# A decoder layer on one core: attention's key copied out of its accumulators by ScalarE, scaled and rotated in SBUF behind the inverse's first update

## The chip, the cores and the metric

The kernel runs on one core of one Trainium2 chip. The metric is the time of one execution on the device in microseconds (us), the median of several runs. Beside the timed runs there is one profiled execution, whose trace gives the start and length of each instruction on each engine: PE (TensorE, matmuls; PEld is its weight load), DVE (VectorE), ACT (ScalarE), POOL (GpSimd) and SP (SyncE, which here issues DMAs). PE writes its results into accumulators in PSUM, eight banks of 128 partitions by 512 float32; DVE and ACT read them there.

## What is computed

One layer of a hybrid decoder on a sequence of 256 tokens of width 1024, in float32. An RWKV-7 branch and a softmax attention branch take the same normalised input and are merged by gates; a gated MLP follows.

```python
h = rms_norm(x, norm1_g)
proj = h @ w_in                                  # one combined projection
y_a = rwkv7_time_mix(token_shift(proj[:RWKV_IN]), ...)
q, k, v = heads of proj[RWKV_IN:RWKV_IN + 3 * 512]     # 8 heads of 64
q = partial_rope(rms_norm(q, q_norm_g), positions)     # rotates 16 of 64 columns
k = partial_rope(rms_norm(k, k_norm_g), positions)
y_b = causal_attention(q, k, v)
x = x + (sigmoid(gate_a) * (y_a @ w_branch_a) + sigmoid(gate_b) * (y_b @ w_branch_b)) @ w_out
x = x + conv_ffn(rms_norm(x, norm2_g), ...)
```

In the RWKV branch a state of 64 by 64 per head is updated for each token by a decay and a rank-one correction. The change touches only the key `k` of the attention, between its projection and its use; what is computed stays the same.

## The kernel before

**Weights.** Every weight tile of 128 by 1024 passes through three steps: SP loads it into `raw` (4 buffers), ACT rounds it into `whi` (L262, a CAST, 4 buffers), DVE takes the rest `wlo` = `raw` - `whi` (L272, 3 buffers). PE multiplies the two halves apart (L300, L302 and L305, or L321, L322 and L325) to keep float32 accuracy. These steps stand in the queues of ACT and DVE between all other work.

**Two threads.** The middle of the kernel is written as generators that a small planner at L1200 interleaves by costs and delays: `bulk` issues the projections, gates and branch products, `chain` the RWKV branch, and `att` the attention (from the moment its inputs are issued). Within an engine instructions run in the order in which they stand in its queue; code inside `tc.high_priority()` is moved ahead of code that isn't, and `tc.issue_after(i)` keeps an instruction behind another in the order.

**The inverse.** The RWKV recurrence is taken in chunks of 64 tokens, for each of which a triangular 64 by 64 matrix is inverted (16 pairs of head and chunk per half of the partitions). The inverses of its 16 by 16 blocks are made on DVE and spread by DMAs into `X0` and, transposed, `X`. Then PE doubles the block size twice. First `pp` = G times X0 (L844), copied to `P` by ACT and DVE (L850, L851); `px` = X times P (L858), added into `X0` on DVE with four instructions (L864): this is the inverse's first update. Then `pxt` (L872), in two halves, gives the same for `X`, which ACT copies (L880); `pp` (L886), `pxt` (L897) make the second doubling. Between these pieces the planner puts gate tiles (L300 to L305) and the attention's transposes (`pqk`, L1052), one piece of work each.

**The key.** `attention_input(i)` projects query (i = 0), value (2) and key (1) into two accumulators of 128 tokens by 512 each. For the key the first comes from the tag `acc` and the second from the tag `ch` (3 buffers), from which `px`, `pxt` and `pp` take theirs too. `finish_qk(p, i, t)` is then called for both halves t of the tokens: ACT squares the accumulator into `s2` (L1016), DVE sums per head into `r2` (L1019), and, for the key, DVE and POOL make the inverse root (L1021, L1022); DVE multiplies the accumulator by it into `qkv` (L1026) and rotates 16 columns by six small instructions (two `ro` at L1035, L1037 and L1038 among them). The accumulator is free when L1026 has read it. `attention()` turns query and key with `pqk` on PE, four transposes at a time, twice for the query and then twice for the key, each time copied out by ACT (L1053).

Of the kernel before, what the change touches and what calls it, by code (L numbers as in the profile page):

```python
# [13 lines left out]
OP = mybir.AluOpType  # L14
# [22 lines left out]
def body(tc, x, positions, norm1_g, w_in, rwkv_mu, w_decay_up, decay_bias, w_aaa_up,  # L37
# [3 lines left out]
    act, dve, pool, pe = nc.scalar, nc.vector, nc.gpsimd, nc.tensor  # L41
    ctx = ExitStack()
    with ctx:
# [12 lines left out]
        def b4(name, shape=(128, 4, 256), dt=F32):  # L56
            return sb.tile(list(shape), dt, name=name, tag="b4", bufs=NB4)
# [53 lines left out]
        rowf = cst.tile([128, 1], F32, name="rowf")  # L111
# [450 lines left out]
        def chain():  # L562
# [45 lines left out]
            p = chp("pss")  # L608
# [15 lines left out]
            for ct in range(4):  # L624
                dve.scalar_tensor_tensor(kk[:, ct], zk[:, ct], col(KK_ + ct), pr[ct],
                                         op0=OP.mult, op1=OP.mult)
# [205 lines left out]
            def quad(side, h):  # L832
                return slice(64 * side + 32 * h, 64 * side + 32 * h + 32)
# [26 lines left out]
            for a in range(2):  # L860
                for q in range(2):
                    v = X0[quad(1 - q, 0), 8 * a:8 * a + 8, 0:16]
                    with tc.high_priority():
                        dve.scalar_tensor_tensor(v, px[a][quad(1 - q, 0)], rowf[quad(1 - q, 0)], v,  # L864
                                                 op0=OP.mult, op1=OP.add)
            yield 0.6, 2.5
            pt = chp("pxt")[:, 0:256].rearrange("p (u n) -> p u n", n=16)
            for h in range(2):
# [136 lines left out]
        qkv = {}  # L1005
        ybs = []
        inv_last = []

        def finish_qk(p, i, t):

            d = qkv[i][:, t]
            if i == 2:
                act.copy(d.rearrange("p h n -> p (h n)"), p)
                return
            s2 = b2("s2", [128, 512])
            act.activation(s2, p, AF.Square)  # L1016
            r2 = sb.tile([128, 8], F32, name="r2", tag="r2", bufs=2)
            with tc.high_priority():
                dve.tensor_reduce(r2, s2.rearrange("p (h n) -> p h n", h=8), axis=AX.X, op=OP.add)  # L1019
                if i:  # L1020
                    dve.tensor_scalar(r2, r2, 1.0 / N, NORM_EPS, op0=OP.mult, op1=OP.add)  # L1021
                    pool.tensor_tensor(r2, r2, eps1[:, 1:2].to_broadcast([128, 8]), op=OP.pow)  # L1022
                else:
                    act.activation(r2, r2, AF.Sqrt, scale=1.0 / N, bias=eps1[:, 0:1])
                    dve.reciprocal(r2, r2)
                dve.tensor_tensor(d, p.rearrange("p (h n) -> p h n", h=8),  # L1026
                                  r2[:, :, None].to_broadcast([128, 8, 64]), op=OP.mult)
            ro = sb.tile([128, 2, 2, 8, HALF], F32, name="ro", tag="ro", bufs=2)
            en = dve
            y = [d[:, :, 0:HALF], d[:, :, HALF:ROT]]  # L1030
            with ExitStack() as st:
                if inv_last:
                    st.enter_context(tc.issue_after(inv_last[-1]))
                for f in range(2):
                    en.tensor_tensor(ro[:, f], y[f][:, None].to_broadcast([128, 2, 8, HALF]),  # L1035
                                     rot[:, i, t, f][:, :, None, :].to_broadcast([128, 2, 8, HALF]), op=OP.mult)
                en.tensor_tensor(y[0], ro[:, 0, 0], ro[:, 1, 0], op=OP.subtract)  # L1037
                en.tensor_tensor(y[1], ro[:, 1, 1], ro[:, 0, 1], op=OP.add)  # L1038
# [4 lines left out]
        def attention():  # L1043
            qkT = []
            for i in range(2):
                dT = b4(f"qkT{i}")
                for j in range(2):
                    p = atp("pqk").rearrange("p (a t c) -> p a t c", a=2, t=2)
                    for a in range(2):
                        for t in range(2):  # L1050
                            ct = 2 * j + a
                            pe.transpose(p[:, a, t], flat3(qkv[i][:, t])[:, ct * 128:ct * 128 + 128], ident)  # L1052
                    act.activation(dT[:, 2 * j:2 * j + 2].rearrange("p a c -> p (a c)"),  # L1053
                                   p.rearrange("p a t c -> p (a t c)"), AF.Copy, scale=gcol[:, i:i + 1])
                    yield 0.4, 1.0
                    while not joined[0] and "chain" not in done:
                        yield 0, 0.1
                qkT.append(dT)
            qT, kT = qkT


            sc0 = by("sc", (128, 8, 128))
            sc1 = cst.tile([128, 2112], F32, name="sc1", tag="KB")[:, 0:2048].rearrange("p (h k) -> p h k", k=256)
            parts = ((0, 0, 8, sc0), (1, 0, 4, sc1[:, 0:4]), (1, 1, 4, sc1[:, 4:8]))

            def scores(t, j, nh, sc):
                nk = 128 * (t + 1)
                ts = slice(t * 128, t * 128 + 128)
                pq = [atp("ps").rearrange("p (h k) -> p h k", k=nk) for q in range(2)]
                for i in range(nh // 2):  # L1070

                    for q, hs in PAR:
                        pe.matmul(pq[q][:, i], qT[hs, 2 * j + i, ts], kT[hs, 2 * j + i, 0:nk],
                                  start=True, stop=True)
                for q in range(2):
                    dve.tensor_tensor(sc[:, q:nh:2, nk - 128:nk], pq[q][:, :, nk - 128:nk],
                                      cmask[:, None, :].to_broadcast([128, nh // 2, 128]), op=OP.add)
                    if t:
                        act.copy(sc[:, q:nh:2, 0:128], pq[q][:, :, 0:128])

            def softmax(t, j, nh, sc):
                nk = 128 * (t + 1)
                mx = sb.tile([128, nh], F32, name="mx", tag="mx", bufs=2)
                dve.tensor_reduce(mx, sc, axis=AX.X, op=OP.max)
                dve.tensor_scalar(mx, mx, -0.125, None, op0=OP.mult)
                sm = sb.tile([128, nh], F32, name="sm", tag="sm", bufs=2)
                for h in range(nh):
                    act.activation(sc[:, h], sc[:, h], AF.Exp, scale=0.125, bias=mx[:, h:h + 1],
                                   accum_out=sm[:, h:h + 1])
                dve.reciprocal(sm, sm)  # L1090
                dve.tensor_tensor(sc, sc, sm[:, :, None].to_broadcast([128, nh, nk]), op=OP.mult)

            def turned_w(t, j, nh, sc):

                pTs = []
                for g in range(2):
                    pp = atp("ppt")
                    pT = b2("pT", [128, 512])
                    for i in range(4):
                        h, b = g * nh // 2 + i // (t + 1), i % (t + 1)  # L1100
                        pe.transpose(pp[:, i * 128:i * 128 + 128], sc[:, h, b * 128:b * 128 + 128], ident)
                    act.copy(pT, pp)
                    pTs.append(pT)
                return pTs

            def weighted(t, pTs):

                po = atp("po").rearrange("p (i c) -> p i c", i=4)
                for ct in range(4):
                    for b in range(t + 1):  # L1110
                        for q, hs in PAR:
                            n = (2 * ct + q) * (t + 1) + b
                            pe.matmul(po[hs, ct], qkv[2][:, b, 2 * ct + q],
                                      pTs[n // 4][:, n % 4 * 128:n % 4 * 128 + 128],
                                      start=ct + b == 0, stop=ct == 3 and b == t, skip_group_check=True)
                hv = ybh[:, :, t * 128:t * 128 + 128]
                act.copy(hv, po)
                dve.tensor_tensor(ybl[:, :, t * 128:t * 128 + 128], po, hv.bitcast(F32), op=OP.subtract)


            for i, part in enumerate(parts):
                scores(*part)
                yield 0.9, 2.5
                softmax(*part)
                while i < 2 and not joined[0] and "chain" not in done:
                    yield 0, 0.1
            yield 0, 4.0
            ybh = by("ybh", dt=F32R)
            ybl = by("ybl", dt=F32R)
            p0 = turned_w(*parts[0])  # L1130
            yield 0.9, 2.5
            weighted(0, p0)
            pa = turned_w(*parts[1])
            yield 1.8, 3.0
            pb = turned_w(*parts[2])
            yield 0.9, 2.5
            weighted(1, pa + pb)
            yield 1.9, 2.5
            ybs.extend((ybh, ybl))
# [254 lines left out]
```

## Time and profile before

| what | value |
|---|---|
| timed runs, median | 409.33 us (409.2 to 409.97, 3 runs) |
| the profiled execution | 410.96 us |
| its span, from first to last instruction | 409.0 us |
| granted TensorE clock, mean over the span | 0.996 of full speed |
| weight CASTs on ACT (L262) | 122 of 1052 ns, 127.8 us |
| weight rests on DVE (L272) | 122 of 1228 ns, 149.4 us |

The span lies 1.96 us below the profiled execution's own time; that rest is ahead of the first and behind the last instruction. A row of a timeline has the start and the length in us, the engine, the line, the operation, its output and inputs, the shape and a count; brackets hold the idle time of the engine just before it and what ended that. In a view of waits the columns are the total in us, how many times, and the longest. The chain of waits is followed back from the last instruction, at each step to what released it. A row of windows has a stretch of the span, its length, the busy time of engines with a count of instructions, the granted clock of TensorE as a share of full speed, the busy share of the DMA engines and GB/s. A row of one line's instructions has the least, the middle and the greatest duration in ns. Buffer numbers are left out of names, so `X` stands for both `X0` and `X`, and `r` and `s` for `r2` and `s2`.

### The profile page before, as it was taken

Reading aid. Unit: us, or ns where it says so; the run is one execution under the profiler, and the core shown is the slowest. Engines: PE = TensorE matmul, PEld = TensorE weight load, DVE = VectorE, ACT = ScalarE, POOL = GpSimd, SP = SyncE. Lnnn points to the kernel's source line nnn. Section 1 sums busy time; section 2 is a strip of 40 time slices with the busy share of each in tenths; the row PEclk is TensorE's granted clock in tenths of the full one; section 3 lists DMA queues with packets and bytes.
Section 4 is the critical chain, followed back from the end, with each engine's and each line's share of the span. In section 5 each row is a group of like instructions: output and inputs, shape, how many; then the busy total and the mean of one; then the engine's idle time right before and its main releaser. Section 6 shows DMA issues by size and latency. Waiting matters only on the chain.

```text
span 409.0 us, 8287 instructions
## 1 busy us (share of the span) xinstructions
PE 401.1 (98%) x3282; PEld 349.6 (85%) x3282; DVE 316.9 (77%) x537; ACT 232.8 (57%) x391; POOL 44.4 (11%) x72
## 2 busy tenths in 40 slices
PE   7999999999989999999999999999999999999996
PEld 3899899887889898999988888888888888888885
DVE  3878999769464798677965898968769678697794
ACT  6999666365436776543554864635545555464450
POOL 8810610213220010000000000000000000000000
PEclk9999999999989999999999999999999999999999
DMA  8973557645825333636665547566655666656612
GB/s 244 325 233 103 169 147 204 163 124 141 223 57 158 101 104 106 206 113 200 192 200 172 159 156 216 190 205 174 222 178 167 209 191 199 195 173 204 198 57 104
DMA packets 60193, 70.35 MB, mean 172 GB/s; under 512 B 7608, under 2 KB 50506, under 8 KB 60154
## 3 DMA queue, kind: packets, MB, share of 16 engines
q1 hardware_dynamic: 59222, 69.40, 57.0%
q0 software_dynamic: 880, 0.41, 0.6%
q8 instruction: 26, 0.43, 0.4%
q14 instruction: 13, 0.11, 0.1%
q10 hardware_dynamic: 52, 0.01, 0.0%
HBM read 68.37 MB, written 1.44 MB: 171 GB/s over the span
## 4 chain that ended last, share of the span: by engine, by line
PE 82%; DVE 6%; DMA 5%; issue 2%; ACT 2%; POOL 1%; SPq 1%; DVEq 0%; ACTq 0%; POOLq 0%
PE acc L1275 20%; PE acc L1280 10%; PE acc L300 7%; PE acc L305 6%; PE acc L302 6%; PE f L1297 4%; PE f L1299 4%; PE f L1295 4%; PE acc L321 3%; PE acc L325 3%; PE acc L322 3%; PE idle L465 1%; DMA raw<-in_w_in_dram 1%; DMA x<-in_x_dram 1%; DMA Tb<-d 1%
## 5 line engine op out<-in xcount | busy, mean ns | idle before, releaser
L262 ACT CAST whi<-raw 128x1024 fp32r<-128x1024 f32 x122 | 127.8, 1052 | 116.5 <-PE acc L1275 40.3
L272 DVE TENSOR_TENSOR wlo<-raw,whi 128x1024 fp32r<-128x1024 f32 x122 | 149.4, 1228 | 40.6 <-PE acc L1280 14.1
L1275 PE MATMUL acc<-hx,whi 128*128 128x512 f32 x352 | 89.5, 395 | 0.0
L1275 PEld LDWEIGHTS acc<-hx,whi 128*128 128x128 f32 x352 | 63.4, 188 | 12.4
L300 PE MATMUL acc<-hx,whi 128*128 128x256 f32 x224 | 57.9, 292 | 0.0
L302 PE MATMUL acc<-hx,whi 128*128 128x256 f32 x224 | 55.4, 282 | 0.0
L1280 PEld LDWEIGHTS acc<-hx,wlo 128*128 128x128 f32 x352 | 46.8, 188 | 4.0
L1280 PE MATMUL acc<-hx,wlo 128*128 128x256 f32 x352 | 47.3, 277 | 0.0
L300 PEld LDWEIGHTS acc<-hx,whi 128*128 128x128 f32 x224 | 43.0, 192 | 2.5 <-issue 1.4
L302 PEld LDWEIGHTS acc<-hx,whi 128*128 128x128 f32 x224 | 42.9, 192 | 0.1
L305 PE MATMUL acc<-hx,wlo 128*128 128x256 f32 x224 | 35.4, 281 | 0.0
L1297 PE MATMUL f<-whi,hb 128*128 128x512 f32 x80 | 31.2, 390 | 0.0
L1299 PE MATMUL f<-wlo,hb 128*128 128x512 f32 x80 | 31.2, 390 | 0.0
L1295 PE MATMUL f<-whi,hb 128*128 128x512 f32 x80 | 31.2, 389 | 0.0
L305 PEld LDWEIGHTS acc<-hx,wlo 128*128 128x128 f32 x224 | 30.4, 191 | 0.0
L1285 DVE TENSOR_REDUCE an<-acc 128x256 f32<-128x512 f32 x22 | 14.2, 686 | 9.4 <-PE acc L1280 9.3
L321 PE MATMUL acc<-whi,hx 128*128 128x512 f32 x48 | 19.5, 406 | 0.0
L322 PE MATMUL acc<-whi,hx 128*128 128x512 f32 x48 | 18.8, 392 | 0.0
L1299 PEld LDWEIGHTS f<-wlo,hb 128*128 128x128 f32 x80 | 15.0, 188 | 3.1
L1297 PEld LDWEIGHTS f<-whi,hb 128*128 128x128 f32 x80 | 15.0, 188 | 2.8
L1295 PEld LDWEIGHTS f<-whi,hb 128*128 128x128 f32 x80 | 15.0, 188 | 2.8
L325 PE MATMUL acc<-wlo,hx 128*128 128x512 f32 x48 | 14.9, 392 | 0.0
(326 smaller groups left out, 621.9 us busy)
## 6 DMA issues: line engine op xcount, KB each, us to landing
raw<-in_w_ffn_up_dram SPq DMA_DIRECT2D x44, 512.0 KB, 4.3
raw<-in_w_in_dram SPq DMA_DIRECT2D x41, 512.0 KB, 4.2
raw<-in_w_ffn_down_dram SPq DMA_DIRECT2D x22, 512.0 KB, 3.4
raw<-in_w_out_dram SPq DMA_DIRECT2D x8, 512.0 KB, 4.5
x<-in_x_dram SPq DMA_DIRECT2D x8, 256.0 KB, 3.9
raw<-in_w_branch_b_dram SPq DMA_DIRECT2D x4, 512.0 KB, 4.2
raw<-in_w_branch_a_dram SPq DMA_DIRECT2D x4, 512.0 KB, 3.5
out_dram<-o SPq DMA_DIRECT2D x3, 256.0 KB
```

What stands on the lines that cost most here:

```text
L262: act.copy(hi[:, :k * c], raw[:, :k * c])
L272: eng.tensor_tensor(lo[:, :n], raw[:, :n], hi[:, :n].bitcast(F32), op=OP.subtract)
L300: pe.matmul(om, wh[:, k, ms], xh[:, k0 + k], start=k0 + k + m == 0, stop=False, skip_group_check=True)
L302: pe.matmul(om, wh[:, k, ms], xl[:, k0 + k], start=False, stop=False, skip_group_check=True)
L305: pe.matmul(om, wl[:, k, ms], xh[:, k0 + k], start=False, stop=k0 + k == nk - 1 and m == n - 1, skip_group_check=True)
L321: pe.matmul(ps_[t], xh[:, K, ts], wh[:, k], start=K == 0, stop=False)
L322: pe.matmul(ps_[t], xl[:, K, ts], wh[:, k], start=False, stop=False)
L1275: pe.matmul(ps_[m], wh[:, k, m * 128:m * 128 + 128], hx[:, k0 + k].rearrange("p a s -> p (a s)"), start=k0 + k == 0, stop=False, skip_grou ...
L1280: pe.matmul(ps_[m][:, 0:S], wl[:, k, m * 128:m * 128 + 128], hh[:, k0 + k], start=False, stop=k0 + k == 7, skip_group_check=True)
L1295: pe.matmul(fin[f], hb[:, 0, i, ts], wh[:, 0, cs], start=st, stop=False, skip_group_check=f == 3)
L1297: pe.matmul(fin[f], hb[:, 1, i, ts], wh[:, 0, cs], start=False, stop=False, skip_group_check=f == 3)
L1299: pe.matmul(fin[f], hb[:, 0, i, ts], wl[:, 0, cs], start=False, stop=False, skip_group_check=f == 3)
```

## The change

For the key, ACT copies each accumulator as it is into `qkv`, right behind the square. The multiply by the inverse root and the rotation are put off: a list `later` keeps them, and `key_scaled()` issues them from `qkv` in SBUF, in place, behind the last of the four instructions of the inverse's first update (or ahead of the key's first turn in `attention()`, if the chain has not come there). The rotation becomes a function of its own; for the query it now stands inside the block with high priority.

```diff
-                        dve.scalar_tensor_tensor(v, px[a][quad(1 - q, 0)], rowf[quad(1 - q, 0)], v,
-                                                 op0=OP.mult, op1=OP.add)
+                        x0_last.append(dve.scalar_tensor_tensor(v, px[a][quad(1 - q, 0)], rowf[quad(1 - q, 0)], v,
+                                                                op0=OP.mult, op1=OP.add).ins)
+            key_scaled()
...
+        later, x0_last = [], []
...
-                dve.tensor_tensor(d, p.rearrange("p (h n) -> p h n", h=8),
-                                  r2[:, :, None].to_broadcast([128, 8, 64]), op=OP.mult)
+                if i:
+                    act.copy(d.rearrange("p h n -> p (h n)"), p)
+                else:
+                    dve.tensor_tensor(d, p.rearrange("p (h n) -> p h n", h=8),
+                                      r2[:, :, None].to_broadcast([128, 8, 64]), op=OP.mult)
+                    rotate(i, t)
+            if i:
+                later.append((t, r2))
+
+        def key_scaled():
+            for t, r2 in later:
+                with tc.issue_after(x0_last[-1]):
+                    dve.tensor_tensor(qkv[1][:, t], qkv[1][:, t], r2[:, :, None].to_broadcast([128, 8, 64]),
+                                      op=OP.mult)
+                rotate(1, t)
+            later.clear()
+
+        def rotate(i, t):
+            d = qkv[i][:, t]
...
             for i in range(2):
+                if i:
+                    key_scaled()
                 dT = b4(f"qkT{i}")
```

On PE nothing moves. What changes there is what the first half of `pxt` waits for, behind the gate tile that uses the accumulator `acc`. Before:

```order
L305 MATMUL acc<-hx,wlo 128x256 x4
L872 MATMUL pxt<-X,P 16x16 [waits DVE_49,Activation_49]
L872 MATMUL pxt<-X,P 16x16 x31
L1052 MATMUL pqk<-ident,qkv 128x128 x4
L300 MATMUL acc<-hx,whi 128x256
```

Now (the lines of the changed kernel lie 1 to 21 further down):

```order
L305 MATMUL acc<-hx,wlo 128x256 x4
L873 MATMUL pxt<-X,P 16x16 [waits Activation_49]
L873 MATMUL pxt<-X,P 16x16 x31
L1073 MATMUL pqk<-ident,qkv 128x128 x4
L300 MATMUL acc<-hx,whi 128x256
```

The wait for DVE, whose last multiply read the accumulator, is gone; the wait for ACT stays and is now for the second copy.

On ACT, behind the copy of `P`, the two squares `s` of the key stood together; `r` and `s` carry their numbers here, one for each half of the tokens. Before:

```order
L850 COPY P<-pp 128x128 [waits PE_49]
L1016 ACTIVATE s_1476<-acc 128x512
L1016 ACTIVATE s_1488<-acc 128x512
L262 CAST whi<-raw 128x1024 [waits DMAHW3_49,DVE_49,PE_49]
L1053 ACTIVATE qkT_1572<-pqk,gcol 128x512 [waits DMASW0_49,DMASW1_49,PE_49,Pool_49]
```

Now:

```order
L850 COPY P<-pp 128x128 [waits PE_49]
L1018 ACTIVATE s_1476<-acc 128x512
L1029 COPY qkv<-acc 128x512
L1018 ACTIVATE s_1483<-acc 128x512
L1029 COPY qkv<-acc 128x512
L262 CAST whi<-raw 128x1024 [waits DMAHW3_49,DVE_49,PE_49]
L1074 ACTIVATE qkT_1574<-pqk,gcol 128x512 [waits DMASW0_49,DMASW1_49,PE_49,Pool_49]
```

Two copies have come in, ahead of the weight CAST and the first turned query.

On DVE, from the inverse root's first scaling to the key's last rotation; `X_1127` is `X0`. Before:

```order
L1021 TENSOR_SCALAR r_1490<-r_1490 128x8 [waits DVE_49]
L1026 TENSOR_TENSOR qkv<-acc,r_1478 128x512 [waits Pool_49]
L1026 TENSOR_TENSOR qkv<-acc,r_1490 128x512 [waits Pool_49]
L1035 TENSOR_TENSOR ro<-qkv,rot 128x128 [waits DVE_49]
L1035 TENSOR_TENSOR ro<-qkv,rot 128x128
L864 SCALAR_TENSOR_TENSOR X_1127<-px,rowf,X_1127 32x8x16 [waits DMASW3_49,PE_49]
...
L1035 TENSOR_TENSOR ro<-qkv,rot 128x128 x2
L272 TENSOR_TENSOR wlo<-raw,whi 128x1024 [waits DMAHW2_49]
L1037 TENSOR_TENSOR qkv<-ro 128x8x8 [waits DVE_49]
L1038 TENSOR_TENSOR qkv<-ro 128x8x8
L272 TENSOR_TENSOR wlo<-raw,whi 128x1024 [waits DMAHW3_49,PE_49,Activation_49]
```

Now:

```order
L1023 TENSOR_SCALAR r_1485<-r_1485 128x8 [waits DVE_49]
L272 TENSOR_TENSOR wlo<-raw,whi 128x1024 [waits DMAHW2_49,PE_49]
L864 SCALAR_TENSOR_TENSOR X_1127<-px,rowf,X_1127 32x8x16 [waits DMASW3_49,PE_49,Pool_49]
...
L1040 TENSOR_TENSOR qkv<-qkv,r_1478 128x512 [waits Pool_49]
L1040 TENSOR_TENSOR qkv<-qkv,r_1485 128x512 [waits Activation_49,Pool_49]
L1054 TENSOR_TENSOR ro<-qkv,rot 128x128 [waits DVE_49]
...
L1054 TENSOR_TENSOR ro<-qkv,rot 128x128
L272 TENSOR_TENSOR wlo<-raw,whi 128x1024 [waits DMAHW3_49,PE_49,Activation_49]
L1056 TENSOR_TENSOR qkv<-ro 128x8x8 [waits DVE_49]
L1057 TENSOR_TENSOR qkv<-ro 128x8x8
```

A weight rest and the four updates of `X0` have moved ahead of the two multiplies, and a second weight rest stands ahead of the last two instructions of the rotation. The update's wait for POOL, new in its row, is for the early clearing of `X0`. At the query, the six instructions of the second half's rotation stand ahead of a shift of `zv` that two of them stood behind.

## The prediction

> **What bounds the kernel now.** I read the page first, then PE's waits, the chain of waits, and the timelines of PE, DVE and ACT around the one place that stands out.
>
> ```profile
> PE 401.1 (98%) x3282; PEld 349.6 (85%) x3282; DVE 316.9 (77%) x537; ACT 232.8 (57%) x391; POOL 44.4 (11%) x72
> PEclk9999999999989999999999999999999999999999
> ```
>
> PE is busy for 98% of the span and its clock drops in one slice only, the twelfth (112.5 to 122.7 us). So time can be won only where PE stands still or runs slowly. The view of PE's own waits, by total us, times and the longest, has three rows and no more:
>
> ```profile
> PE xt L426 <- DVE xn L419: 1.6, 2, 0.8
> PE pxt L872 <- DVE qkv L1026: 1.5, 1, 1.5
> PE idle L387 <- DVE eps L382: 1.5, 1, 1.5
> ```
>
> The first and third lie in the first 9 us. The second is the only named wait after the start: the first matmul of `pxt` (L872) waits for the multiply L1026 that scales the attention key out of its accumulator, since `pxt` takes over that accumulator's bank. The chain of waits shows how the multiply comes to be late:
>
> ```profile
> 108.64 1.05 ACT whi L262
> 109.69 0.16 ACT P L850
> 109.85 0.51 ACT s L1016
> 110.38 1.28 DVE r L1019 x2
> 111.83 3.30 POOL r L1022 x2
> 115.15 0.70 DVE qkv L1026
> ```
>
> Square on ACT, two sums on DVE, two powers in a row on POOL (3.30 us), then the second multiply, which ends at 115.85. PE had come to `pxt` at 114.50:
>
> ```profile
> 115.99 0.97 PE L872 MATMUL pxt<-X,P 32*16 32x16 f32 x64 [1.49 <-DVE qkv L1026]
> 116.89 0.98 PE L1052 MATMUL pqk<-ident,qkv 128*128 128x128 f32 x4
> 117.52 0.56 PE L300 MATMUL acc<-hx,whi 128*128 128x256 f32 x1
> ...
> 121.86 0.97 PE L872 MATMUL pxt<-X,P 32*16 32x16 f32 x64
> 122.75 0.66 PE L1052 MATMUL pqk<-ident,qkv 128*128 128x128 f32 x4
> 123.17 0.36 PE L300 MATMUL acc<-hx,whi 128*128 128x256 f32 x1
> ...
> 126.09 0.75 PE L886 MATMUL pp<-X,G 32*32 32x32 f32 x64
> ```
>
> The same three pieces (one half of `pxt`, four turns `pqk`, one gate weight tile) stand there twice. The first set takes 121.86 - 115.99 = 5.87 us, the second 126.09 - 121.86 = 4.23. The windows say why:
>
> ```profile
> 116.00:117.00 1.00, 1.00 (x65) 1.00 0.00 0
> 117.00:118.00 1.00, 1.00 (x6) 0.54 0.06 16
> 118.00:119.00 1.00, 1.00 (x7) 0.50 0.00 0
> 119.00:120.00 1.00, 1.00 (x6) 0.50 0.00 0
> 120.00:121.00 1.00, 1.00 (x8) 0.75 0.63 52
> ```
>
> The columns are stretch, length, PE busy, granted clock, DMA share and GB/s. The clock is halved from 117.0 to about 120.5; its loss is 0.46 + 0.50 + 0.50 + 0.25 = 1.71 us, close to 5.87 - 4.23 = **1.64**, which I use. So this wait costs **1.49 us idle and, in this execution, 1.64 us of clock behind it**.
>
> **The change, part by part.** *The wait goes.* The accumulators are now read by four ACT instructions in a row, square, copy, square, copy, and `pxt` waits for ACT alone. The copy of this shape from an accumulator exists already for the value, and the squares start 0.49 us apart:
>
> ```profile
> L1013 ACT COPY qkv<-acc x2: 580/583/586, 83.1 to 85.0; 128x512 f32<-128x512 f32 x2
> 109.75 1.09 ACT L1016 ACTIVATE s<-acc 128x512 f32<-128x512 f32 x2
> ```
>
> Four steps of 0.49 from 109.75 and a last tail end the second copy near 111.8. PE wants the bank at 114.50: 2.7 us to spare. Minus 1.49 us. No table load is added between square and copy.
>
> *The clock dip goes with it.* From 114.5 PE then has a half of `pxt`, four turns and dense tiles without a gap, as at 121.86 to 126.09, where no slot of the clock row shows a loss. Minus 1.64.
>
> *ACT, two copies more.* They delay what is queued behind them, two weight CASTs with a turned query between:
>
> ```profile
> 110.71 1.06 ACT L262 CAST whi<-raw 128x1024 fp32r<-128x1024 f32 x1
> 114.08 1.04 ACT L262 CAST whi<-raw 128x1024 fp32r<-128x1024 f32 x1 [1.55 <-PE acc L302]
> ```
>
> The delay is 2 x 0.49 = 1 us, and it ends at the second CAST, ahead of which ACT sat idle 1.55 us for PE. The first CAST feeds a weight tile that PE reaches two tiles after `pxt`. So it costs nothing; without that cover it would cost the 1 us.
>
> *DVE, new order.* What decides is when the key is scaled and rotated, since PE turns it (third `pqk`, at 122.75 now). The rows:
>
> ```profile
> 110.38 1.28 DVE L1019 TENSOR_REDUCE r<-s 128x8 f32<-128x512 f32 x2 [2.03 <-ACT s L1016]
> 115.76 0.48 DVE L1035 TENSOR_TENSOR ro<-qkv,rot 128x128 f32<-128x128 f32 x2
> 116.28 1.23 DVE L864 SCALAR_TENSOR_TENSOR X<-px,rowf,X 32x128 f32<-32x128 f32 x4
> 117.43 0.20 DVE L1037 TENSOR_TENSOR qkv<-ro 128x64 f32<-128x64 f32 x1
> 118.10 1.21 DVE L272 TENSOR_TENSOR wlo<-raw,whi 128x1024 fp32r<-128x1024 f32 x1
> L1022 POOL TENSOR_TENSOR r<-r,eps x2: 1633/1652/1672, 111.8 to 113.5; 128x8 f32<-128x8 f32 x2
> L1026 DVE TENSOR_TENSOR qkv<-acc,r x4: 627/680/691, 61.4 to 115.2; 128x512 f32<-128x512 f32 x4
> L1091 DVE TENSOR_TENSOR sc<-sc,sm x3: 1216/1226/1228, 139.9 to 153.4; 128x1024 f32<-128x1024 f32 x3
> ```
>
> The second sum now waits for a square that starts 0.49 later, so both sums and their scalings end near 112.2. A weight split `wlo` (1.21) comes next, whose operands are there, to 113.3; then the four updates of the inverse (1.23), to 114.5. The powers follow their own sums: 111.2 + 1.65 = 112.9 and + 1.65 = 114.5, so neither multiply waits for POOL by more than a moment. A multiply of this shape from SBUF is not in the trace: 0.69 is the same multiply from the accumulator (L1026), 0.61 is half of the softmax's in-place multiply of twice the width (L1091). I take 0.69, the row of the same length; two of them run to about 115.8. Then come three of the four rotations `ro` (0.26 each: two from 115.76 to the update at 116.28), two combinations, the fourth `ro`, a second `wlo` and the last two combinations: 115.8 + 0.8 + 0.3 + 0.3 + 1.1 + 0.3 = **118.6**, or 118.4 at the low price of the multiplies. PE arrives at the third `pqk` at 114.5 + 5.1, namely its half of `pxt`, turns, tile (4.23) and second half (0.89): 114.50 + 4.23 + 0.89 = **119.6**. The key is ready 1.0 to 1.2 us early. Cost nothing; if that margin is gone, each us late costs one us.
>
> *The updates of the inverse* start at 113.3 in place of 116.28; their reader (L886 at 126.09) did not wait, so nothing is won. The weight split moved ahead of them frees a weight buffer 5 us sooner; PE waits for no load there, so nothing either. POOL and SP keep their order. *The query's rotation*, at 62 to 65 us, moves two small combinations ahead of a `zv` shift, about 0.3 us by their spacing above; PE has no wait in that stretch: nothing.
>
> *Does the gain reach the end?*
>
> ```profile
> 121.00:225.00 104.00, 103.86 (x1169) 94.33 (x1169) 76.31 (x132) 60.04 (x125) 4.93 (x4) 1.00 0.52 157
> 225.00:400.00 175.00, 175.00 (x939) 150.04 (x938) 142.64 (x213) 95.18 (x138) 0.70 (x1) 1.00 0.59 181
> ACT whi L262 <- PE acc L1275: 40.3, 28, 1.8
> ```
>
> After 121 us PE is idle for 0.14 us up to 400, DMA is half used, and the weight CASTs wait for PE, not the other way round. A PE that runs 3 us earlier pulls all of it along.
>
> Sum: 1.49 + 1.64 = 3.13 us, on the profiled execution 410.96 (span 409.0 and 1.96 around it): 407.8. That execution lies 1.63 us above the median of the timed runs, 409.33. On the median the sum gives **406.2**. But 1.63 is also just the size of the clock term, and that leaves a doubt: the profiled execution may have had a dip that the timed ones do not have.
>
> **The rivals.** *Only the wait goes.* The dip begins a full microsecond after PE has resumed, so it is granted by some count over a stretch whose phase I do not see; the idle 1.49 us and tiny matmuls fell together in 113.6 to 117.0 here. If the timed runs have no dip, or it also comes without the wait, the gain is 1.49: **407.8**. For it: the 1.63 us between profile and median. Against it: three timed runs within 0.8 us, and no dip behind the later `pxt` and turns.
>
> By the Trainium skill, page "TensorE: Matmul & The Clock Gate", Part 1 on the clock gate, the clock halves after an idle window of about 3.4 us, in a window that runs free of the kernel. The length of the dip, 117.0 to 120.5, agrees with such a window; its cause does not, since 1.49 us idle came before it. By that rule the wait had not been long enough, and the sum would be 1.49 alone, as in this rival.
>
> *A new wait takes the place of the old one, and the kernel is slower.* The place is the third `pqk`: between the key's two rotations DVE now has a weight split that waits for its load and its CAST, and behind it the last rotation. Were that held for W us beyond PE's arrival at 119.6, PE would pay W, and from about 1.5 us on the clock dip of 1.64 again. It passes the old time when W + 1.64 is over 3.13, so from W = 1.5: the key ready at 121.1, 2.5 us later than worked out. At W = 2.5 the time is 406.2 + 2.5 + 1.64 = **410.3**. Against it: that CAST ran at 110.71 already, so its load had landed, and POOL is done by 114.5.
>
> *The change does not do what it says*: `pxt` stands at the same place because of something else that becomes ready near 116, or the gain is taken back before 225 us. Then **409.3**. Against it: the copies are done 2.7 us ahead, and the view of PE's waits has nothing later.
>
> **How the numbers follow.** Both terms go: 0.53, at 406.2 (its own range 405.5 to 407.0). Only the wait: 0.29, at 407.8. No effect: 0.11, at 409.3. Slower: 0.07, at 410.3. The range 405.5 to 408.3 takes in the first two cases and leaves out 0.18; the low end allows 0.7 for the multiplies' price and the spread of runs. A difference of 0.2%, 0.8 us, is about what a measurement can tell: faster than 408.5 has 0.83, between that and 410.1 0.11, slower 0.06.
>
> **What would show it.** Right: PE has no wait at `pxt` and the clock row shows no slot below 9; the first `pxt` starts within 0.1 of the end of the tile ahead of it; the second copy on ACT ends near 112; the last key combination on DVE ends near 118.6, PE's third `pqk` starts near 119.6; the span is about 405.9. Wrong: a wait of PE on the key's combination at the third `pqk`; a dip of the clock that stays although the wait is gone (the second term falls); or a later idle time of PE of about the size won.

## The result and the profile after

The changed kernel takes **407.67 us** (median of 22 runs, 406.48 to 408.66). The kernel before, run beside it 22 times, takes 409.76 (407.39 to 412.80). The ratio is **0.9946, with a 95% interval of 0.9930 to 0.9963**: faster by 0.54%, or 2.1 us between the medians. The profiled execution took 407.20 us, with a span of 405.1 and a mean granted clock of 1.000; before it was 410.96, 409.0 and 0.996.

The page of the changed kernel, its engines and its row of the granted clock:

```profile
PE 399.6 (99%) x3282; PEld 347.9 (86%) x3282; DVE 316.9 (78%) x537; ACT 233.8 (58%) x393; POOL 44.6 (11%) x72
...
PEclk9999999999999999999999999999999999999999
...
PE 98%; DMA 1%; DVE 0%; issue 0%; ACT 0%; SPq 0%
```

No slot of the clock is below 9 now, and the third line, the chain of work by engine, is 98% PE. The whole view of PE's waits (total us, times, longest):

```profile
PE idle L387 <- DVE eps L382: 1.5, 1, 1.5
PE xt L426 <- DVE xn L419: 0.7, 1, 0.7
```

Both lie in the start-up. The wait at `pxt` is gone, and nothing has taken its place. The timeline of PE from the inverse's first update to the second doubling:

```profile
109.80 0.73 PE L858 MATMUL px<-P,X 32*32 32x16 f32 x64
...
113.78 0.97 PE L873 MATMUL pxt<-X,P 32*16 32x16 f32 x64
114.68 0.66 PE L1073 MATMUL pqk<-ident,qkv 128*128 128x128 f32 x4
...
118.00 0.97 PE L873 MATMUL pxt<-X,P 32*16 32x16 f32 x64
118.90 0.66 PE L1073 MATMUL pqk<-ident,qkv 128*128 128x128 f32 x4
...
122.22 0.75 PE L887 MATMUL pp<-X,G 32*32 32x32 f32 x64
```

From the first `pxt` to the second PE now takes 4.22 us, as from the second to `pp`; before, the first of these stretches took 5.87. From `px` to `pp` it takes 12.42 us. Before it took 15.65, from `px` at 110.44 to `pp` at 126.09, so 3.23 us are gone here. The other 0.64 us of the 3.9 by which the span is shorter lie ahead of `px` (110.44 against 109.80). Of these, 0.37 come from the start-up (its first gate tile, L300, starts at 17.76 before and at 17.39 now; the waits of `xt` there were 1.6 us and are 0.7), the rest in small parts between 102 and 110 us, all of it ahead of the key's first copy (109.95).

ACT and DVE in the same place:

```profile
108.35 1.05 ACT L262 CAST whi<-raw 128x1024 fp32r<-128x1024 f32 x1 [5.02 <-DMA raw<-in_w_in_dram]
109.31 0.26 ACT L850 COPY P<-pp 128x128 f32<-128x128 f32 x1
109.46 0.60 ACT L1018 ACTIVATE s<-acc 128x512 f32<-128x512 f32 x1
109.95 0.59 ACT L1029 COPY qkv<-acc 128x512 f32<-128x512 f32 x1
110.42 0.62 ACT L1018 ACTIVATE s<-acc 128x512 f32<-128x512 f32 x1
110.91 0.61 ACT L1029 COPY qkv<-acc 128x512 f32<-128x512 f32 x1
```

```profile
111.87 1.22 DVE L272 TENSOR_TENSOR wlo<-raw,whi 128x1024 fp32r<-128x1024 f32 x1
113.13 1.22 DVE L864 SCALAR_TENSOR_TENSOR X<-px,rowf,X 32x128 f32<-32x128 f32 x4
114.28 1.27 DVE L1040 TENSOR_TENSOR qkv<-qkv,r 128x512 f32<-128x512 f32 x2
...
117.83 0.20 DVE L1057 TENSOR_TENSOR qkv<-ro 128x64 f32<-128x64 f32 x1
```

The second copy ends at 111.52, 2.26 us ahead of `pxt`. The two multiplies from SBUF take 1.27 us together, 0.64 each, between the two bounds of 0.61 and 0.69. The key is ready at 118.03, and PE turns it at 118.90: 0.87 us to spare.

So in the two profiled executions the place itself went as worked out, 3.23 us for 3.13. In the timed runs the gain is 2.1. The first row of ACT above points to the reason, and the kernel before has the same row, of which the prediction did not follow the wait. Here it is, with the piece of the chain of waits that stands ahead of the pieces shown there:

```profile
103.09 5.44 DMA raw<-in_w_in_dram
```

```profile
108.64 1.05 ACT L262 CAST whi<-raw 128x1024 fp32r<-128x1024 f32 x1 [4.94 <-DMA raw<-in_w_in_dram]
```

ACT stood idle for 4.94 us on the load of a weight tile. The copy of `P` and the key's squares, whose inputs were there, stood behind that CAST in ACT's queue. The chain that ended in the wait at `pxt` began with a load.

### The profile page after: what moved, and what is told of

The parts are those of the page before. It is cut to its first block, busy times and chain, and to the rows that moved or that the text cites. A ratio compares the mean times of both kernels' runs of the same rounds, so it can differ in the third digit from the quotient of the medians.

```text
span 405.1 us, 8289 instructions
## 1 busy us (share of the span) xinstructions
PE 399.6 (99%) x3282; PEld 347.9 (86%) x3282; DVE 316.9 (78%) x537; ACT 233.8 (58%) x393; POOL 44.6 (11%) x72
## 4 chain that ended last, share of the span: by engine, by line
PE 98%; DMA 1%; DVE 0%; issue 0%; ACT 0%; SPq 0%
PE acc L1296 20%; PE acc L1301 10%; PE acc L300 9%; PE acc L302 8%; PE acc L305 8%; PE acc L321 5%; PE acc L325 5%; PE acc L322 5%; PE f L1318 5%; PE f L1316 4%; PE f L1320 4%; PE idle L465 1%; PE pgr L681 1%; DMA x<-in_x_dram 1%; PE ppt L1122 1%; PE ps L1094 1%
## 5 line engine op out<-in xcount | busy, mean ns | idle before, releaser
L262 ACT CAST whi<-raw 128x1024 fp32r<-128x1024 f32 x122 | 127.8, 1051 | 114.4 <-PE acc L1296 39.5
L1296 PEld LDWEIGHTS acc<-hx,whi 128*128 128x128 f32 x352 | 63.4, 188 | 12.4
L300 PE MATMUL acc<-hx,whi 128*128 128x256 f32 x224 | 56.9, 289 | 0.0
L302 PE MATMUL acc<-hx,whi 128*128 128x256 f32 x224 | 54.6, 279 | 0.0
L300 PEld LDWEIGHTS acc<-hx,whi 128*128 128x128 f32 x224 | 42.2, 188 | 2.5 <-issue 1.4
L302 PEld LDWEIGHTS acc<-hx,whi 128*128 128x128 f32 x224 | 42.2, 189 | 0.1
```

The lines of the kernel that those rows point to most:

```text
L262: act.copy(hi[:, :k * c], raw[:, :k * c])
L300: pe.matmul(om, wh[:, k, ms], xh[:, k0 + k], start=k0 + k + m == 0, stop=False, skip_group_check=True)
L302: pe.matmul(om, wh[:, k, ms], xl[:, k0 + k], start=False, stop=False, skip_group_check=True)
L1296: pe.matmul(ps_[m], wh[:, k, m * 128:m * 128 + 128], hx[:, k0 + k].rearrange("p a s -> p (a s)"), start=k0 + k == 0, stop=False, skip_grou ...
```

## The experiments

Three sets of runs. The first and the third ran on one chip, the second on another; on which chip the comparison above ran is not known. In the expectations A is the prediction's account: the wait of 1.49 us is always there, and the clock falls because of it. E, formed after the first set, is the late load. The other accounts are told where they are named.

### First set: which part of the change does it, and what does a wait cost

**Copies without the deferral.** The accumulators are copied as in the changed kernel, but multiply and rotation stay where they were, reading SBUF.

```diff
-                dve.tensor_tensor(d, p.rearrange("p (h n) -> p h n", h=8),
-                                  r2[:, :, None].to_broadcast([128, 8, 64]), op=OP.mult)
+                if i:
+                    act.copy(d.rearrange("p h n -> p (h n)"), p)
+                    src = d
+                else:
+                    src = p.rearrange("p (h n) -> p h n", h=8)
+                dve.tensor_tensor(d, src, r2[:, :, None].to_broadcast([128, 8, 64]), op=OP.mult)
```

> The two copies alone: the accumulator is freed by ScalarE, the key is scaled in SBUF as soon as its power is there, and nothing is put off by hand. Theory A (the wait costs 1.49 us in every execution, the halved clock 1.64 us more only in some executions): no wait at the first pxt, clock 1.00 in all runs, the same time as the changed kernel, about 2.1 us below the kernel before. Theory B (both terms are lost in every execution, and 1 us is given back by putting the multiply off): 3.1 us below. Theory C (the deferral itself made the gain): no gain.

**The second half first, no copies.** The key's halves are finished in the other order, so that the accumulator which `pxt` takes over is read first.

```diff
-                for t in range(2):
+                for t in (1, 0) if i == 1 else (0, 1):
```

> No copies at all. The two halves of the key are finished in the other order, so that the half whose bank pxt takes gets its power and its multiply first, 1.65 us sooner. Theory A: the multiply ends near 114.2 on the scale of the profile of before, PE comes at 114.5 and does not wait; clock 1.00 in all runs; about 2.1 us below the kernel before, the same as the changed kernel. Theory B with the give-back in ScalarE's two copies: 3.1 us below. Theory C (the copies and the new order matter, not the wait): no gain.

**One more power.** The kernel before, with an unused power on POOL ahead of the second half's own: the wait is to grow by its 1.65 us.

```diff
+                    if t:
+                        r3 = sb.tile([128, 8], F32, name="r3")
+                        pool.tensor_tensor(r3, r2, eps1[:, 1:2].to_broadcast([128, 8]), op=OP.pow)
```

> The kernel before with one more power on GpSimd (1.65 us, its result unused) ahead of the second half's power: PE's wait at pxt grows from 1.49 to about 3.14 us. Theory A: the clock is halved in nearly every run (mean clock 0.996 or less in most), and the time grows by 1.65 us and by the share of the 1.64 us that the kernel before did not pay, together about 2.6 us above the kernel before. Theory B (the clock is always halved already): 1.65 us above. Theory D (the timed runs see no halved clock): 1.65 us above with a clock of 1.00.

**A short wait.** Halves in the other order and an unused power of half the width in front.

```diff
-                    pool.tensor_tensor(r2, r2, eps1[:, 1:2].to_broadcast([128, 8]), op=OP.pow)
+                    with ExitStack() as st:
+                        if t:
+                            r3 = sb.tile([128, 4], F32, name="r3")
+                            pool.tensor_tensor(r3, r2[:, 0:4], eps1[:, 1:2].to_broadcast([128, 4]), op=OP.pow)
+                        else:
+                            st.enter_context(tc.issue_after(pow_last[-1]))
+                        pow_last.append(pool.tensor_tensor(r2, r2, eps1[:, 1:2].to_broadcast([128, 8]), op=OP.pow).ins)
...
-                for t in range(2):
+                for t in (1, 0) if i == 1 else (0, 1):
```

> As the run with the second half first, with a power of half the width (1.0 us by its row, its result unused) ahead of that half's power: PE's wait at pxt is about 0.75 us. Theory A: the clock is halved in fewer runs than in the kernel before, or in none; 0.75 us plus at most a small share of 1.64 above the run with no wait, so about 1.2 us below the kernel before. Theory B (any wait here halves the clock): 0.75 + 1.64 above the run with no wait, 0.7 us below the kernel before or no gain.

Measured, beside a kernel before that took **407.51** here (33 runs), not 409.76:

| kernel | median us | against before, 95% | PE's wait at `pxt` in its profile |
|---|---|---|---|
| copies, no deferral | 407.72 | 0.9999 (0.9990 to 1.0008) | none |
| second half first | 407.45 | 0.9992 (0.9975 to 1.0010) | none |
| one more power | 409.13 | 1.0038 (1.0021 to 1.0056) | 1.31 |
| a short wait | 407.56 | 1.0002 (0.9991 to 1.0013) | 1.20 |

On this chip the kernel before was as fast as the changed one had been, and the copies alone, or the other order of the halves, won nothing. That is the number of C, and A and B both missed; but C's reason does not follow, since the whole change wins nothing here either (the second and third set show it). The extra power shows why. In its profile, PE's wait at `pxt` is

```profile
PE pxt L872 <- DVE qkv L1029: 1.3, 1, 1.3
```

1.31 us, where an addition of 1.65 to 1.49 had been expected to give 3.14. By that estimate PE would not have waited here without the power, by 1.65 - 1.31 = 0.34 us. **A's fixed wait fell at this run.** (The time lies 409.13 - 407.51 = 1.62 us above the kernel before, where B and D had said 1.65. That agreement is luck: both had started from a wait of 1.49 in every run.) The CAST ahead of the squares, in the timeline of the same kernel, says what was different:

```profile
106.13 1.05 ACT L262 CAST whi<-raw 128x1024 fp32r<-128x1024 f32 x1 [2.76 <-DMA raw<-in_w_in_dram]
```

It starts at 106.13, where before's profile has 108.64. The short wait gives the other case. Its profiled execution took 410.57 us, and all its 12 other runs took 406.86 to 408.61. In that one execution:

```profile
108.93 1.05 ACT L262 CAST whi<-raw 128x1024 fp32r<-128x1024 f32 x1 [5.37 <-DMA raw<-in_w_in_dram]
```

The same load, late again, and a wait with it. (The view of waits names a gate of ACT there, but the multiply of the second half ends at 115.60, 0.15 us ahead of `pxt` at 115.75, the same step as from 115.84 to 115.99 in before's profile. 0.75 us had been expected, for an early load.) The time from the load's issue on SP to the CAST is 5.55 us in the profile of before, 5.66 in that of the changed kernel and 6.16 here. In the other three of this set it is 4.10, 4.07 and 4.06. That is theory E: **the kernel before waits at `pxt` in executions in which this one load lands late, and in no others.** So far it rests on these profiles, one of each kernel.

### Second set: the load made late on purpose

Four spare scatters of 16 KB, of data that nothing uses, are put in SP's queue right ahead of the load, in the kernel before and in the changed one:

```diff
+            spare = sb.tile([128, 16, 16], F32, name="spare")
+            for b in range(4):
+                nc.sync.dma_start(spare[16 * b:16 * b + 16], d3[2 * b].rearrange("q u (i n) -> i (q u) n", i=16))
```

> The kernel before with four more scatters of 16 KB, into a spare tile, in SyncE's queue ahead of that weight load (their data are not used): the load is issued about 1.9 us later, so its CAST on ScalarE starts near 108.3 where it would start near 106.2. Theory E: PE's wait at pxt appears in most runs, 1.2 to 2 us, with the halved clock in some; median 1.5 to 3 us above a kernel before whose load is early. Theory A: the load is not what the wait hangs on; no change beyond 0.3 us.

> The changed kernel with the same four scatters ahead of the weight load. Theory E: the copies end 2.7 us ahead of PE, so a load that is 2 us late is still hidden; no wait at pxt, at most a few tenths at px, whose operand is copied behind the same CAST; 1.5 to 3 us below the kernel before with the late load, within 0.5 us of the changed kernel without it. Theory A: the same as the changed kernel.

The third kernel is before with the same scatters and no copies. The weight CASTs that stood ahead of the copy of `P` and of the squares are put behind them in ACT's queue:

```diff
-        def split_hi():
+        def split_hi(after=None):
...
+                with ExitStack() as st:
+                    if after:
+                        st.enter_context(tc.issue_after(after[-1]))
...
-            act.activation(s2, p, AF.Square)
+            sq_last.append(act.activation(s2, p, AF.Square).ins)
...
-                yield from xst(ps_, hh, hl)
+                yield from xst(ps_, hh, hl, hold=i == 1)
...
+                if i == 1:
+                    split_hi(sq_last)
```

(`hold` keeps back the last tile's CAST until the squares are issued.)

> The kernel before with the late load, and no copies: instead ScalarE's CAST of that weight tile and the one ahead of it stand behind the copy of P and the key's two squares. Theory E: the key's chain no longer waits for the load; squares near 107 us on PE's scale, no wait at pxt though the load is as late as in the other two runs; the time of the changed kernel. If the wait is still there, something other than the load's place in ScalarE's queue holds the squares.

And the changed kernel once more as it is:

> The changed kernel once more, beside the kernel before on the chip of this call. Theory E (new: the wait of 1.49 us is there only when one weight tile lands late, near 108.4 us of the span, and gone when it lands near 106.2): the gain depends on how often the load is late here; 2.1 us as in the first comparison where most executions of the kernel before span over 407 us, and nothing where they span 405 to 406. Theory A (the wait is always there): 1.5 us at least, on any chip.

The kernel before took 407.65 us on this chip (29 runs, 406.28 to 410.59).

| kernel | median us (range) | against before, 95% |
|---|---|---|
| before, late load | 411.93 (410.69 to 412.53) | 1.0110 (1.0089 to 1.0131) |
| changed, late load | 408.43 (406.80 to 409.19) | 1.0025 (1.0008 to 1.0043) |
| before, late load, CASTs behind | 408.13 (407.17 to 408.53) | 1.0013 (1.0002 to 1.0025) |
| changed, as it is | 407.60 (407.07 to 408.05) | 1.0000 (0.9983 to 1.0016) |

The kernel before with its load made late has the wait again, now in its profile and, by time and clock, in all six runs. The profile, first PE's wait, then PE's row, then the windows behind it (PE busy, granted clock, DMA share and GB/s):

```profile
PE pxt L874 <- DVE qkv L1028: 2.0, 1, 2.0
```

```profile
115.45 0.97 PE L874 MATMUL pxt<-X,P 32*16 32x16 f32 x64 [1.96 <-DVE qkv L1028]
```

```profile
116.00:117.00 1.00, 1.00 (x38) 0.82 0.06 16
117.00:118.00 1.00, 1.00 (x7) 0.50 0.00 0
118.00:119.00 1.00, 1.00 (x7) 0.50 0.00 0
119.00:120.00 1.00, 1.00 (x6) 0.50 0.06 13
120.00:121.00 1.00, 1.00 (x11) 0.97 1.01 238
```

1.96 us of wait and 0.18 + 3 x 0.50 + 0.03 = 1.71 us of clock: 3.67. All six of its runs have a mean granted clock of 0.996. They lie 4.3 us above the kernel before, where 1.5 to 3 had been expected, and the clock fell in all, not in some. The same delay in the changed kernel, ACT and PE:

```profile
109.53 1.05 ACT L262 CAST whi<-raw 128x1024 fp32r<-128x1024 f32 x1 [5.50 <-DMA raw<-in_w_in_dram]
...
112.08 0.61 ACT L1031 COPY qkv<-acc 128x512 f32<-128x512 f32 x1
```

```profile
110.79 0.80 PE L860 MATMUL px<-P,X 32*32 32x16 f32 x64 [0.23 <-ACT P L852]
...
114.85 1.16 PE L875 MATMUL pxt<-X,P 32*16 32x16 f32 x64
```

The second copy ends at 112.69, still 2.16 us ahead of `pxt`, PE does not wait there, only 0.23 us at `px`, and the runs' clocks are 0.999 or 1.000. Between the two medians lie 411.93 - 408.43 = **3.5 us**: where the load is late, the change is worth about what the prediction gave it, 3.13. With the CASTs behind the squares and no copies the loss is gone too, 3.8 us below the first. Both stay 0.5 to 0.8 us above this set's changed kernel without scatters (407.60). For the changed kernel with them at most 0.5 had been expected, and it is 0.8; where the scatters cost that was not followed. The third kernel's timeline of ACT, and PE's row:

```profile
107.75 0.27 ACT L855 COPY P<-pp 128x128 f32<-128x128 f32 x1 [6.08 <-PE pp L849]
107.92 1.09 ACT L1022 ACTIVATE s<-acc 128x512 f32<-128x512 f32 x2
108.88 2.00 ACT L264 CAST whi<-raw 128x1024 fp32r<-128x1024 f32 x2
```

```profile
114.63 0.97 PE L877 MATMUL pxt<-X,P 32*16 32x16 f32 x64
```

`P` and the squares follow PE, not the load, which was issued at 105.05 (the quickest load in this stretch took 4.4 us to land). That settles the way from the load to the wait, with the same scatters in all three kernels: it goes through the CAST in ACT's queue. The changed kernel as it is took the time of before, 1.0000, as E said for a kernel before whose runs are short: the load was early in its own profile (the CAST at 106.66) and, by their times, in nearly all runs of before.

### Third set: can anything be won where the load is early

The same CASTs behind the squares without the scatters; the kernel before with the scatters of L770 that SP issues given to POOL, so that the load goes out at 101.22; and the changed kernel a third time.

```diff
-                    both[b % 2].dma_start(
+                    nc.gpsimd.dma_start(
```

> The kernel before with the two weight CASTs behind the copy of P and the key's squares, no other change. Theory E: squares at 107 us, no wait at pxt in any execution, the same time as the changed kernel within 0.2%, on a chip with early loads the same as the kernel before too. If holding the CASTs back costs PE a weight tile: 0.5 us or more above the changed kernel.

> The kernel before with SyncE's last four scatters given to GpSimd's queue, so that the weight load is issued right behind the first four, near 101 us in place of 102 to 103. Theory E: the load lands 1 to 2 us sooner and its CAST starts near 104.5 to 106 in every execution; no wait at pxt; the same time as the changed kernel within 0.2%. If the scatters that GpSimd now issues come too late for px: a wait there, 0.5 us or more above.

> The changed kernel a third time, on whatever chip this call is given. Theory E: where most executions of the kernel before span 405 to 406 us there is no gain; where they span over 407, some 2 us. Theory A: a gain of 1.5 us at least on any chip.

The kernel before took 407.71 us (29 runs). CASTs behind: 407.47, 0.9992 (0.9980 to 1.0005). Load ahead of the scatters: 407.84, 1.0004 (0.9993 to 1.0016). Changed: 407.47, 0.9999 (0.9984 to 1.0014). The first two lie within 0.2% of the changed kernel, as E had said. No profile of the three has a wait of PE at `pxt`. The second of them has before's order of the key's work, and shows by how little it gets by when the load is early. Its CAST came at 106.51, not between 104.5 and 106, because now it waited for PE, no longer for the load:

```profile
106.51 1.05 ACT L262 CAST whi<-raw 128x1024 fp32r<-128x1024 f32 x1 [2.58 <-PE acc L322]
```

On DVE and PE:

```profile
113.16 0.69 DVE L1026 TENSOR_TENSOR qkv<-acc,r 128x512 f32<-128x512 f32 x1 [0.93 <-POOL r L1022]
```

```profile
114.49 0.97 PE L872 MATMUL pxt<-X,P 32*16 32x16 f32 x64
```

The multiply ends at 113.85, and PE comes at 114.49: 0.64 us to spare, where the profile of before is late by 115.84 - 114.50 = 1.34. No kernel was measurably faster than the changed one: with no wait left there is nothing more to win at `pxt`.

The four comparisons of the two kernels, as medians:

| comparison | before | runs of before over 409.0 | changed |
|---|---|---|---|
| the result | 409.76 | 18 of 22 | 407.67 |
| first set | 407.51 | 1 of 33 | not run |
| second set | 407.65 | 2 of 29 | 407.60 |
| third set | 407.71 | 2 of 29 | 407.47 |

The changed kernel takes the same time in its three comparisons. What varies is the kernel before. That the load was late in most of its 22 runs in the result is read from their times: only one execution of the kernel before was profiled, and its load was late; 409.0 is about 407.5 plus the wait alone, so the count is rough.

## Why the prediction was right in kind and off in size

- **The wait goes: right.** The second copy was to end near 111.8 and ends at 111.52; `pxt` starts without a wait, also with a load that is late by design.
- **The clock dip goes with it: right.** It was gone in the profile of the changed kernel, came back with the wait in the profile of the kernel before with a late load and in the clocks of all its six runs, and was away in the changed one with the same delay.
- **Their size in one execution: right.** 3.23 us against 3.13 in the profiled executions, 3.5 between the medians of the runs with the load made late.
- **The step that failed** is the sum's last one, which put "1.49 + 1.64 = 3.13 us" on the median of the timed runs. The sum was mis-sized there: 2.1 us in the result, 0.05 and 0.24 between the medians of the second and third set, both within their intervals. An execution of before pays it only when the load is late. That 407.67 lies in the stated 405.5 to 408.3 all the same is in part luck: no term of the sum stands for a mix of executions with and without the wait. The error began earlier, in the chain of waits: it was shown from "108.64 1.05 ACT whi L262" on, as square, sums, powers and multiply, without the 4.94 us that ACT had waited for the load ahead of it. This wait hangs on a transfer, and it varied with the transfer.
- **The doubt named there** saw that the profiled execution lay 1.63 above the median, and looked for it in the clock alone. By the experiments the wait itself varies as well, and the clock with it. The executions of before over 409.0 in the result have a median of 410.27, 2.6 us above the changed kernel. That lies between the wait alone and wait and clock together; the clocks of those runs were not recorded, so how many had the dip stays open.
- **Rival "only the wait goes", 407.8:** its number is the nearest to 407.67, its reason is not what the runs show. The clocks of the timed runs with a late load show the dip, and it goes with the wait. The 2.1 us lie between medians over executions that paid different amounts, as far as their times tell.
- **Rival "a new wait at the third `pqk`":** did not come, with 0.87 us to spare (1.0 to 1.2 was worked out). **Rival "no effect":** false as it was meant, since nothing else holds `pxt`; yet where the load is early the change has no effect, for a reason that was not among the rivals: there is no wait to remove.
- **Costs put at nothing: right.** With the load early, the copies with and without the deferral both took the time of before (0.9999 and 1.0000, intervals up to 0.17% wide to a side, 0.7 us), so neither ACT's two copies nor DVE's new order shows in the time.

**What stays open** is why this load lands late in most executions of one comparison and in a few of the others. The chip, its neighbours or the time of day may do it, and none was varied alone. Transfers beside it in the profiles differ, but not in a way that separates the two cases in all of them.

## What to carry to other kernels

Follow a wait back past the first engine that looks like its cause, to the end of the idle time ahead of it; if a DMA stands there, the wait may be absent in other executions, as here, and several executions are to be looked at before it is priced. In a queue that runs in order, an instruction that waits for a load should stand behind short work that others wait for: here that took 3.8 us off under the late load, with no copies at all. A change that makes a kernel insensitive to a late transfer is worth its full price only where the transfer is late, so its gain has to be quoted with the comparison that it was measured in.

## What the runs showed of the chip

**A short wait can halve the clock.** Of the kernel with one more power, the windows behind its wait of 1.31 us:

```profile
116.00:117.00 1.00, 1.00 (x18) 0.69 0.06 16
117.00:118.00 1.00, 1.00 (x7) 0.50 0.00 0
118.00:119.00 1.00, 1.00 (x7) 0.50 0.00 0
119.00:120.00 1.00, 1.00 (x7) 0.61 0.35 32
```

At half the clock for (0.31 + 0.50 + 0.50 + 0.39) / 0.50 = 3.4 us, and by the same sum 3.42 behind the wait of 1.96. The windows of before and of the short wait give 3.42 too. So it is one stretch of one length behind waits of 1.20 to 1.96 us. Of the 13 profiles here it is in the four that have a wait at `pxt`, and in no other. In the timed runs it does not come each time. Of the ten runs of this kernel two have the mean clock of 0.996 that such a stretch gives; of the five runs of before over 409.0 in the three sets it is two (0.994 and 0.995). With the late load made on purpose (1.96 us in the profile) it was six of six. A run of this kernel of 410.42 us and one of before of 410.59 have 1.000: if a wait made them 2.9 us longer than the median of before, it was a longer one and passed without the stretch, but neither run has a profile. By the Trainium skill, page "TensorE: Matmul & The Clock Gate", Part 1 on the clock gate, the clock halves after an idle window of about 3.4 us that runs free of the kernel. The length of 3.4 agrees. That an idle time of that length is needed does not: 1.31 us were enough here in some runs. Chance in the shorter waits fits a window that runs free; no run here moved a wait against it.

**One load, several landing times.** The same 512 KB load took 4.0 to 4.1 us from its issue to the CAST that waited for it in four profiles, 5.6 to 6.2 in three others, and 4.60 and 4.84 behind the spare scatters. The changed kernel alone has both: 102.69 to 108.35 in its first profile, 5.66 us, and 4.02 in the second set. The rows there, of SP's issues (the first of the three is this load's) and of the CAST:

```profile
102.64 2.13 SPq L250 DMA_DIRECT2D raw<-in_w_in_dram  x3
```

```profile
106.66 1.05 ACT L262 CAST whi<-raw 128x1024 fp32r<-128x1024 f32 x1 [2.94 <-DMA raw<-in_w_in_dram]
```
